# Six of eight output-projection chunks as three pairs of seven block products

## The chip, the cores and the metric

The kernel runs on one core of one Trainium2 chip. The metric is the device time of one execution in microseconds, as the median of three runs.

## The reference, cut to what matters

Two decoder layers work on `x` of 1024 tokens by 1024 features, all in float32. The part of a layer that the change touches is the output projection of the mixer and the addition to the residual stream, between the gated merge and the second RMSNorm:

```python
merged = g_a * (o_a @ w_br[l, :OUT_A]) + g_b * (o_b @ w_br[l, OUT_A:])
x = x + merged @ w_o[l]            # w_o[l] is 1024 x 1024
h2 = rmsnorm(x, norm2[l])
up = h2 @ w_up[l]
```

## The kernel before

Activations lie transposed: features on the 128 partitions, tokens along the free axis. The tokens are cut into two halves `n` = 0 and 1 of 512, the 1024 features into eight chunks of 128 (`k` on the input side, `e` on the output side). A float32 product is made of three float32r matmuls: every operand is split into a high part (`hh`, `w_hi`, cast by ScalarE at line 129) and a low part (`hl`, `w_lo`, the rest, subtracted by VectorE at line 130), and TensorE adds high times high, high times low and low times high in PSUM. A chunk of 128 output features for 512 tokens is therefore 8 times 3 = 24 matmuls of 128x512.

The merged activations are made by the loop at the end of `mixer`: for each of 16 (n, e) VectorE forms `mrg` (line 1279), ScalarE casts it into `hh` and GpSimd subtracts the low part into `hl` (`merged`, lines 1237 and 1238). Then comes the output projection: `wo_chunk` runs for the eight chunks of n = 0 and then for the eight of n = 1. It loads the chunk's weights in two pieces of 128x512, has them split, lets TensorE make 24 matmuls into a PSUM tile `o_ps`, adds the tile into `x` on VectorE (line 1128) and adds the square of the new `x` to the sum `nrm` for the RMSNorm (`norm_add`: ScalarE squares; VectorE adds for e = 1, 4 and 7, GpSimd for the others).

`norm(0, ...)` is the RMSNorm of the first half: four matmuls by ones give `nrm_t`, ScalarE takes the root, VectorE the reciprocal, four matmuls spread it over the partitions (`nrm_b`), and then for each of eight chunks VectorE scales `x` (line 479), ScalarE casts and VectorE or GpSimd subtracts the low part. `drive` weaves this into the chunks: 36 steps of `wo_chunk` run first (nine chunks), and 2.5 steps run for each step of the norm. The second half's norm is woven into the first products of the feed-forward network (`u_ps`).

TensorE's instructions stand in the order in which the program is written; on the other engines and on SyncE, which issues the DMAs, a scheduler sets the order at build time. On the chip every engine takes its own queue strictly in order. Buffers are rings with fixed counts: the split pieces `w_hi` and `w_lo` four each, raw weights `w_raw` two, the PSUM tag `ps` two, the temporaries of 128x512 (`mrg`, `sq` and others) six.

The feed-forward network and the q, k, v and gate projections already use a scheme of seven block products in place of eight (`seven`, lines 886 to 893, twelve matmuls a product); their sums of weight blocks are made by GpSimd (lines 1011 to 1018 in `pair_rest`), and three-step sums of activations as well (`block_sums`, lines 912 to 914).

Of the kernel before, what the change touches and what calls it, by code (L numbers as in the profile page):

```python
# [52 lines left out]
def trunk_kernel(ctx, tc, x, norm1, w_in, b_gate, w_br, w_o, norm2, w_up, conv_w, conv_b, w_down, norm_f, out, depth=None, probe=None):  # L53
# [62 lines left out]
    def bank(tag, name):  # L116
        return ps.tile([P, 512], F32, tag=tag, name=name)
# [15 lines left out]
    def weights(src, cols, place=None):  # L133

        per = 512 // cols
        got = []
        src = src.rearrange("(k p) n -> p k n", p=P)
        for r in range(0, KD, per):
            raw = sb.tile([P, per, cols], F32, tag="wr", bufs=NRAW, name="w_raw")
            nc.sync.dma_start(raw, src[:, r : r + per, :])  # L140
            if place:
                hi, lo = (x.rearrange("p (k c) -> p k c", c=cols)[:, r : r + per, :] for x in place)
            else:
                hi = sb.tile([P, per, cols], F32R, tag="wh", bufs=4, name="w_hi")
                lo = sb.tile([P, per, cols], F32R, tag="wl", bufs=4, name="w_lo")
            split(hi, lo, raw)
            got += [(hi[:, i, :], lo[:, i, :]) for i in range(per)]
        return got

    def product(o, pairs, first=True, last=True, share=False):  # L150

        n = len(pairs)
        quantum = 2 * 512 // o.shape[-1]
        for i, ((lh, ll), (rh, rl)) in enumerate(pairs):
            pe.matmul(o, lh, rh, start=(first and i == 0), stop=False, skip_group_check=share)  # L155
            pe.matmul(o, lh, rl, start=False, stop=False, skip_group_check=share)  # L156
            pe.matmul(o, ll, rh, start=False, stop=(last and i == n - 1), skip_group_check=share)  # L157
            if i % quantum == quantum - 1 and i < n - 1:
                yield
# [217 lines left out]
    def h_part(n, k):  # L377
        return H[n][0][:, k, :], H[n][1][:, k, :]
# [30 lines left out]
    def norm_add(n, e, first=False, sub=slice(0, HF), adds=None):  # L409

        if first:
            ACC[n] = sb.tile([P, HF], F32, tag="ql", bufs=2, name="nrm")
        acc = ACC[n]
        acc = acc[:, sub]
        sq = acc if first else small("sq")[:, sub]
        act.activation(sq, xc(n, e, sub), AF.Square)
        if not first:
            (adds or (dve if e % 3 == 1 else pool)).tensor_tensor(acc, acc, sq, ALU.add)
# [701 lines left out]
        return pair(dense, l, (OFF_G + e * P, OFF_G + D + e * P), False, put)  # L1120


    def wo_chunk(l, n, e):
        w = weights(w_o[l][:, e * P : (e + 1) * P], P)
        yield
        o = bank("ps", "o_ps")
        yield from product(o, [(w[k], h_part(n, k)) for k in range(KD)])
        dve.tensor_tensor(xc(n, e), xc(n, e), o, ALU.add)
        norm_add(n, e, e == 0)
        yield  # L1130

    def residual_in():

# [12 lines left out]
    def mixer(l, pending):  # L1146
# [79 lines left out]
        def branch_in(i):  # L1226
            if i < len(todo):
# [5 lines left out]
                    split(*parts_[q], raw[:, 2 * q : 2 * q + 2, :])  # L1233
                wbs.append(parts_)

        def merged(n, e, m):
            act.copy(H[n][0][:, e, :], m)
# [3 lines left out]
        wo = [wo_chunk(l, n, e) for n in range(2) for e in range(KD)]  # L1241

        for i in range(3):
            gate_in(i)
# [10 lines left out]
        for i, ab in order:  # L1255
            n, e = todo[i]
            sl = slice(n * HF, (n + 1) * HF)
            if i not in seen:
                if e == 0:
                    new_h(n)  # L1260
                if i % 4 == 0:
                    wb = wbs.pop(0)
                if l and i in X_AT:
                    x_in(X_AT.index(i) // 2, X_AT.index(i) % 2)
            gt = gts[i]
            ec = slice((e % 2) * P, (e % 2 + 1) * P)
# [12 lines left out]
            dve.tensor_tensor(m, gt[:, 0, :], gt[:, 1, :], ALU.add)  # L1279
            late.append((n, e, m))  # L1280
            if i == 11:
                next(wo[0])
# [8 lines left out]
            pass  # L1291
        table(AF.Sqrt, gt[:, 1, 0:1])
        S.clear()

        def first_half():
# [579 lines left out]
```

## Time and profile before

| | |
|---|---|
| runs | 2716.20, 2717.23, 2718.05 us; median 2717.23 us |
| the profiled execution | 2714.47 us, its span 2712.6 us, so 1.9 us lie around the span |
| TensorE | busy 2657.8 us of the span (98%), granted clock 0.997 |
| weight loads beside the matmuls | 2227.5 us (82%) |
| VectorE, ScalarE, GpSimd | 2105.9 (78%), 1330.4 (49%), 742.1 us (27%) |
| output projection, layer 0 | first matmul at 629.1 us, the last chunk added at 718.38 us |
| output projection, layer 1 | first matmul at 1969.34 us, last 2058.0 us |

Busy time is a sum over instructions; matmuls overlap, so the pace of TensorE is read from the distance of events, not from the duration of one matmul. A row of the timeline names the start, the duration, the engine, the line and the tiles, and in brackets how long the engine had been idle and for whom.

### The profile page before, as it was taken

How to read it: one execution, taken by the hardware profiler on the slowest of the kernel's cores; microseconds unless marked ns; L12 is line 12 of the kernel's file. 1: busy time of each engine (PE TensorE's matmuls, PEld its weight loads, DVE VectorE, ACT ScalarE, POOL GpSimd, SP SyncE). 2: the span in 40 equal slices, each digit the busy share in tenths (PEclk: the TensorE clock that was granted, in tenths of full speed). 3: DMA queues.
4: the chain of work that ended last, by engine and by line, in shares of the span. 5: the costliest groups of instructions: out<-in, count | busy, mean ns of one | idle time of the engine just before them, and what ended most of it. 6: DMA issues, size and time to landing. Idle time of an engine off the chain costs nothing. (4 is left out here: it accounts for less than half of the span.)

```text
span 2712.6 us, 37003 instructions
## 1 busy us (share of the span) xinstructions
PE 2657.8 (98%) x13098; PEld 2227.5 (82%) x13098; DVE 2105.9 (78%) x3104; ACT 1330.4 (49%) x2458; POOL 742.1 (27%) x537
## 2 busy tenths in 40 slices
PE   8999999999999999999999989999999999999999
PEld 8877788888888888888888778888788888888888
DVE  6877876675789988897658888766858888998865
ACT  5656534464455555432335665434545545554225
POOL 2004133322233434321220041332212433443210
PEclk9999999999999999999999999999999999999999
DMA  4023389863235444688401234997722444446863
GB/s 153 20 80 123 123 229 246 207 226 121 85 117 171 141 154 147 223 320 320 154 32 36 84 111 136 250 230 211 248 85 79 148 152 143 171 141 253 333 246 122
DMA packets 397637, 445.72 MB, mean 164 GB/s; under 512 B 21660, under 2 KB 318988, under 8 KB 395916
## 3 DMA queue, kind: packets, MB, share of 16 engines
q1 hardware_dynamic: 397452, 443.35, 51.4%
q8 instruction: 104, 1.70, 0.3%
q14 instruction: 81, 0.66, 0.1%
HBM read 300.61 MB, written 142.67 MB: 163 GB/s over the span
## 5 line engine op out<-in xcount | busy, mean ns | idle before, releaser
L130 DVE TENSOR_TENSOR w_lo<-up_a,w_hi 128x512 fp32r<-128x512 f32 x240 | 237.2, 995 | 20.5 <-ACT w_hi L129 20.5
L129 ACT CAST w_hi<-up_a 128x512 fp32r<-128x512 f32 x240 | 149.5, 623 | 184.1 <-PE u_a L890 45.6
L1631 DVE TENSOR_TENSOR x<-x,d_ps 128x512 f32<-128x512 f32 (+1 forms) x228 | 152.2, 672 | 76.9 <-PE d_ps L1625 76.0
L1362 POOL TENSOR_TENSOR cv<-cv 128x512 f32<-128x512 f32 x88 | 132.1, 1513 | 248.8 <-DVE cv L1357 138.9
L130 DVE TENSOR_TENSOR w_lo<-w_raw,w_hi 128x512 fp32r<-128x512 f32 x176 | 132.5, 756 | 67.8 <-ACT w_hi L129 67.3
L129 ACT CAST w_hi<-w_raw 128x512 fp32r<-128x512 f32 x176 | 109.2, 621 | 125.9 <-PE o_ps L156 68.6
L129 ACT CAST w_hi<-in_a 128x512 fp32r<-128x512 f32 x140 | 86.8, 620 | 147.6 <-PE i_a L890 83.2
L130 DVE TENSOR_TENSOR g<-cv,g 128x512 fp32r<-128x512 f32 x154 | 152.4, 991 | 5.2 <-ACT g L129 2.7
L1623 PE MATMUL d_ps<-gd_in,w_hi 128*128 128x512 f32 (+1 forms) x340 | 130.2, 383 | 1.3 <-ACT w_hi L129 1.1
L1625 PE MATMUL d_ps<-gd_in,w_lo 128*128 128x512 f32 (+1 forms) x340 | 129.8, 382 | 0.0
L1624 PE MATMUL d_ps<-gd_in,w_hi 128*128 128x512 f32 (+1 forms) x340 | 129.7, 382 | 0.0
L889 PE MATMUL u_a<-hh,w_hi 128*128 128x512 f32 x320 | 124.7, 390 | 0.5 <-DVE u L1513 0.5
L889 PE MATMUL u_a<-t_hi,w_hi 128*128 128x512 f32 x320 | 124.6, 389 | 0.0
L891 PE MATMUL u_a<-t_hi,w_lo 128*128 128x512 f32 x320 | 124.5, 389 | 0.0
L890 PE MATMUL u_a<-hl,w_hi 128*128 128x512 f32 x320 | 124.5, 389 | 0.0
L891 PE MATMUL u_a<-hh,w_lo 128*128 128x512 f32 x320 | 124.5, 389 | 0.0
L890 PE MATMUL u_a<-t_lo,w_hi 128*128 128x512 f32 x320 | 124.5, 389 | 0.0
L130 DVE TENSOR_TENSOR w_lo<-in_a,w_hi 128x512 fp32r<-128x512 f32 x140 | 116.0, 828 | 4.1 <-ACT w_hi L129 3.7
L1018 POOL TENSOR_TENSOR in_a<-in_a 128x512 f32<-128x512 f32 x28 | 38.0, 1357 | 278.9 <-DVE w_lo L130 278.9
L627 DVE TENSOR_TENSOR_SCAN stay<-stay,zero 128x128 f32<-128x128 f32 (+3 forms) x64 | 89.0, 1390 | 32.2 <-ACT stay L625 31.6
L1623 PE MATMUL d_ps<-gd_in,wd 128*128 128x512 f32 (+1 forms) x292 | 113.9, 390 | 0.0
L129 ACT CAST g<-cv 128x512 fp32r<-128x512 f32 x154 | 95.0, 617 | 38.2 <-POOL cv L1362 29.7
(390 smaller groups left out, 8747.7 us busy)
## 6 DMA issues: line engine op xcount, KB each, us to landing
gd<-g SPq DMA_DIRECT2D x154, 512.0 KB, 3.7
gd_in<-gd SPq DMA_DIRECT2D x154, 512.0 KB, 6.4
up_a<-in_w_up_dram SPq DMA_DIRECT2D x80, 512.0 KB, 5.8
in_a<-in_w_in_dram SPq DMA_DIRECT2D x56, 512.0 KB, 6.2
w_raw<-in_w_in_dram SPq DMA_DIRECT2D x104, 256.0 KB, 3.0
t_kq<-tk SPq DMA_DIRECT2D x64, 384.0 KB, 7.8
wd_raw<-in_w_down_dram SPq DMA_DIRECT2D x22, 1024.0 KB, 13.0
gin<-gs SPq DMA_DIRECT2D x32, 512.0 KB, 4.4
```

What stands on the lines that cost most here:

```text
L129: act.copy(hi, src)
L130: dve.tensor_tensor(lo, src, f32(hi), ALU.subtract)
L627: dve.tensor_tensor_scan(rev, rev, zero[:, 0:1].to_broadcast([P, L]), 1.0, ALU.mult, ALU.add)
L889: pe.matmul(o, w[0][:, c], rh, start=(first and i == 0), stop=False, skip_group_check=True)
L890: pe.matmul(o, w[0][:, c], rl, start=False, stop=False, skip_group_check=True)
L891: pe.matmul(o, w[1][:, c], rh, start=False, stop=(last and i == 3), skip_group_check=True)
L1018: pool.tensor_tensor(a11, a22, a11, ALU.subtract)
L1362: return lambda: pool.tensor_tensor(dst, a, b, ALU.subtract)
L1623: pe.matmul(o[:, sub], wh[:, c], gh[:, sub], start=(i == 0 and k in (0, 4, 5)), stop=False, skip_group_check=True)
L1624: pe.matmul(o[:, sub], wh[:, c], gl[:, sub], start=False, stop=False, skip_group_check=True)
L1625: pe.matmul(o[:, sub], wl[:, c], gh[:, sub], start=False, stop=(i == m - 1), skip_group_check=True)
L1631: dve.tensor_tensor(x, x, o[:, sub], ALU.add)
```

## The change

`output_products` replaces `wo_chunk`. Chunks 0 to 5 are taken as three pairs (2p, 2p+1). A pair for both halves of the tokens is a product of 2 by 2 blocks (512 input features by 128 output features each), made of seven products of twelve matmuls in place of eight. Chunks 6 and 7 stay plain. Every product is added from PSUM into each `x` chunk to which it belongs, so a product may be added twice.

Sums of weight blocks (`weight_sums`, four per pair) are made by GpSimd. Sums of activation blocks (`merged_sums`) are made in four rounds: the first while the activations are merged (GpSimd, in `merged`), the second and the fourth by VectorE, the third by GpSimd in three steps for each of four blocks; each round is then split into a high and a low part on ScalarE and VectorE. A `plan` hangs these tasks on the numbers of the products. The products stand in the order of `items`, numbered from 0: six halves of chunks 6 and 7 (0 to 5), then p1 and p3 of pairs 0 and 1 (6 to 9), p2 (10, 11), p5, p6 and so on to 22; this is `early`, which runs before the first half's norm. The six of `rest` (p2 of pair 2, the three p4, and the second half's chunk 7) are woven into that norm at 0.7 steps a step, with none ahead. The first half's sum `nrm` shares one buffer with the second's. The pieces of weights of an item are prepared three items ahead.

```diff
+    def output_products(l, sums):
+        b11, b12, b21, b22 = (lambda n=n, k=k: half(n, k) for k in range(2) for n in (1, 0))
+        def load_pairs():
+            for p in range(3):
+                if p < 2:
+                    t = [sb.tile([P, 2, HF], F32, tag="p4", bufs=4, name="wo_c") for _ in range(2)]
+                else:
+                    both = sb.tile([P, 4, HF], F32, tag="ql", bufs=2, name="wo_p")
+                    t = [both[:, 0:2, :], both[:, 2:4, :]]
...
+        def weight_sums(p):
+            a11, a12, a21, a22 = tiles[p]
+            pool.tensor_tensor(a21, a21, a22, ALU.add)
+            pool.tensor_tensor(a11, a21, a11, ALU.subtract)
+            pool.tensor_tensor(a12, a12, a11, ALU.subtract)
+            pool.tensor_tensor(a22, a22, a11, ALU.subtract)
+        def add(n, e, o, full=False):
+            dve.tensor_tensor(xc(n, e), xc(n, e), o, ALU.add)
+            if full:
+                norm_add(n, e, e == 6)
...
+        def p3(p):
+            items.append((("tile", p, 1), free("o_3"), p, b22, True, True, lambda o: add(0, 2 * p, o)))
+        def p5(p):
+            def done(o):
+                add(0, 2 * p + 1, o)
+                add(0, 2 * p, o, p == 2)
+            items.append((("tile", p, 2), free("o_5"), p, lambda: S[1], True, True, done))
+        def p7(p):
+            items.append((("tile", p, 3), again, p, lambda: S[3], False, True, lambda o: add(0, 2 * p + 1, o, True)))
...
+        chunk(0, 6)
+        chunk(0, 7)
+        chunk(1, 6)
+        for f, p in ((p1, 0), (p3, 0), (p1, 1), (p3, 1), (p2, 0), (p2, 1)):
+            f(p)
+        for f, p in ((p5, 0), (p6, 0), (p5, 1), (p6, 1), (p1, 2), (p7, 0), (p3, 2), (p7, 1), (p6, 2), (p5, 2), (p7, 2)):
+            f(p)
+        count = len(items)
+        for f, p in ((p2, 2), (p4, 0), (p4, 1), (p4, 2)):
+            f(p)
+        chunk(1, 7)
...
+        def prepare(i):
+            kind, c, k = items[i][0]
+            ready[i] = piece(loaded.pop(i) if kind == "raw" else tiles[c][k])
+            if kind == "tile" and k == 0 and items[i][4]:
+                weight_sums(c)
...
+        def run(first, last):
+            for i in range(first, last):
+                until("fetch", fetch, i + 5)
+                until("prepare", prepare, i + 3)
+                for f in sums.pop(i, ()):
+                    f()
...
+        def third(i):
+            r, (ah, al), (bh, bl) = small("h_sum"), half(0, 1)[i], half(0, 0)[i]
+            pool.tensor_tensor(r, f32(al), f32(bl), ALU.subtract)
+            pool.tensor_tensor(r, r, f32(ah), ALU.add)
+            pool.tensor_tensor(r, r, f32(bh), ALU.subtract)
...
+        for i in range(4):
+            task(i // 2, lambda i=i: split_into(1, i, keep[i]))
+            task(2 + i, second, i)
+            task(6 + 2 * i, third, i)
+            task(8 + 2 * i, lambda i=i: split_into(3, i, third_r[i]))
+            task(16 + i, fourth, i)
+            task(22, lambda i=i: split_into(4, i, keep[i]))
...
         def merged(n, e, m):
+            if e < 4:
...
+                    pool.tensor_tensor(sums[e], kept.pop((0, e)), kept.pop((1, e)), ALU.subtract)
...
-        drive(first_half(), relay(*wo, primed=True), 2.5, 36)
+        start, early, rest = output_products(l, merged_sums(sums))
+        start()
+        for _ in early():
+            pass
...
+        drive(first_half(), rest(), 0.7)
```

Three places of the instruction order show what the build makes of it, all in layer 0. The first is GpSimd's queue at the start of the output projection. Before, the last low parts of the merge are followed only by sums for the norm:

```order
L1238 TENSOR_TENSOR hl0_5946<-mrg_6378,hh0_5945 128x512
L1238 TENSOR_TENSOR hl0_5946<-mrg_6408,hh0_5945 128x512
L1238 TENSOR_TENSOR hl1_5964<-mrg_6436,hh1_5963 128x512
L1238 TENSOR_TENSOR hl1_5964<-mrg_6462,hh1_5963 128x512
L418 TENSOR_TENSOR nrm_6514<-nrm_6514,sq_6595 128x512
L418 TENSOR_TENSOR nrm_6514<-nrm_6514,sq_6636 128x512
```

Now the weight sums of pairs 0 and 1 (`wo_c_6471` and `wo_c_6472` are chunks 0 and 1, `wo_c_6475` and `wo_c_6476` chunks 2 and 3) and the third round (`h_sum`) stand there in one row:

```order
L1149 TENSOR_TENSOR wo_c_6472<-wo_c_6472,wo_c_6471 128x512
L1271 TENSOR_TENSOR h_sum_6655<-hl0_5946 128x512
L1271 TENSOR_TENSOR h_sum_6701<-hl0_5946 128x512
L1272 TENSOR_TENSOR h_sum_6655<-h_sum_6655,hh0_5945 128x512
L1272 TENSOR_TENSOR h_sum_6701<-h_sum_6701,hh0_5945 128x512
L1273 TENSOR_TENSOR h_sum_6655<-h_sum_6655,hh0_5945 128x512
L1273 TENSOR_TENSOR h_sum_6701<-h_sum_6701,hh0_5945 128x512
L1271 TENSOR_TENSOR h_sum_6743<-hl0_5946 128x512
L1147 TENSOR_TENSOR wo_c_6475<-wo_c_6476,wo_c_6475 128x512
L1272 TENSOR_TENSOR h_sum_6743<-h_sum_6743,hh0_5945 128x512
L1148 TENSOR_TENSOR wo_c_6475<-wo_c_6475 128x512
L1149 TENSOR_TENSOR wo_c_6476<-wo_c_6476,wo_c_6475 128x512
```

Ahead of these twelve stand L1147 and L1148 of `wo_c_6471`, of which the first overwrites the block that product 6 is split from. The eleventh row here, L1148 of `wo_c_6475`, makes the block that product 9 (p3 of pair 1) multiplies by; from L1147 of `wo_c_6471` to it are thirteen sums, eight of them of the third round, and the second row after it is the last `h_sum_6743`.

The second place is VectorE's queue around the same products. Before, a chunk has two splits, an addition from `o_ps` and sometimes a sum for the norm:

```order
L1128 TENSOR_TENSOR x0_5939<-x0_5939,o_ps_6528 128x512
L130 TENSOR_TENSOR w_lo_6566<-w_raw_6563,w_hi_6565 128x512
L418 TENSOR_TENSOR nrm_6514<-nrm_6514,sq_6554 128x512
L130 TENSOR_TENSOR w_lo_6601<-w_raw_6598,w_hi_6600 128x512
L1128 TENSOR_TENSOR x0_5939<-x0_5939,o_ps_6569 128x512
L130 TENSOR_TENSOR w_lo_6607<-w_raw_6604,w_hi_6606 128x512
L130 TENSOR_TENSOR w_lo_6642<-w_raw_6639,w_hi_6641 128x512
L1128 TENSOR_TENSOR x0_5939<-x0_5939,o_ps_6610 128x512
```

Now the low parts of the third round (`t_lo_6698` from `h_sum`), parts of the fourth (`m_sum`, L1278 and L1279), the additions from PSUM (L1152) and the splits of weights alternate; `o_ps_6609` is product 5's tile, `o_3_6679` product 7's, `w_lo_6676` belongs to product 9, `w_lo_6694` to product 10:

```order
L130 TENSOR_TENSOR t_lo_6698<-h_sum_6701,t_hi_6697 128x512
L1279 TENSOR_TENSOR m_sum_6074<-m_sum_6074,hl1_5964 128x512
L1152 TENSOR_TENSOR x1_5942<-x1_5942,o_ps_6609 128x512
L130 TENSOR_TENSOR w_lo_6676<-wo_c_6475,w_hi_6675 128x512
L130 TENSOR_TENSOR t_lo_6698<-h_sum_6743,t_hi_6697 128x512
L1278 TENSOR_TENSOR m_sum_6074<-hh1_5963,m_sum_6074 128x512
L1152 TENSOR_TENSOR x1_5941<-x1_5941,o_a_6659 128x512
L130 TENSOR_TENSOR w_lo_6694<-w_raw_6645,w_hi_6693 128x512
L1279 TENSOR_TENSOR m_sum_6074<-m_sum_6074,hl1_5964 128x512
L1278 TENSOR_TENSOR m_sum_6208<-hh1_5963,m_sum_6208 128x512
L1278 TENSOR_TENSOR m_sum_6242<-hh1_5963,m_sum_6242 128x512
L1152 TENSOR_TENSOR x0_5939<-x0_5939,o_3_6679 128x512
```

The addition of product 7's tile, which frees its PSUM bank, has moved behind the split of `h_sum_6743`, and that waits for two more sums on GpSimd.

The third place is TensorE's queue around the first half's norm. Before, `nrm_t` stands in the middle of the second half's chunk 1:

```order
L157 MATMUL o_ps_6856<-hh1_5963,w_lo_6806 128x512
L155 MATMUL o_ps_6856<-hh1_5963,w_hi_6805 128x512
L156 MATMUL o_ps_6856<-hl1_5964,w_hi_6805 128x512
L157 MATMUL o_ps_6856<-hh1_5963,w_lo_6806 128x512
L465 MATMUL nrm_t_6869<-ones_71,nrm_6514 128x1 x4
L155 MATMUL o_ps_6856<-hh1_5963,w_hi_6811 128x512
L156 MATMUL o_ps_6856<-hl1_5964,w_hi_6811 128x512
```

Now it stands right behind the last matmul of product 22, the last that adds into the first half:

```order
L893 MATMUL o_a_6881<-t_hi_6697,w_lo_6964 128x512
L891 MATMUL o_a_6881<-t_hi_6697,w_hi_6963 128x512
L892 MATMUL o_a_6881<-t_lo_6698,w_hi_6963 128x512
L893 MATMUL o_a_6881<-t_hi_6697,w_lo_6964 128x512
L467 MATMUL nrm_t_7037<-ones_71,nrm_6547 128x1 x4
L891 MATMUL o_2_7048<-hh1_5963,w_hi_6982 128x512
L892 MATMUL o_2_7048<-hl1_5964,w_hi_6982 128x512
```

What was a chunk and a half of the other half between the last addition into the first half and `nrm_t` is gone from there.

More of the change, by code (lines that the diff above doesn't have):

```diff
@@ L411, in norm_add @@
         if first:
-            ACC[n] = sb.tile([P, HF], F32, tag="ql", bufs=2, name="nrm")
+            if n == 0 or ACC[0] is None:
+                both = sb.tile([P, 2, HF], F32, tag="ql", bufs=2, name="nrm")
+                ACC[0], ACC[1] = both[:, 0, :], both[:, 1, :]
         acc = ACC[n]
@@ L1240, in mixer @@
         residual = residual_in() if l == 0 else iter(())
-        wo = [wo_chunk(l, n, e) for n in range(2) for e in range(KD)]
         for i in range(3):
@@ L1280, in mixer @@
             late.append((n, e, m))
-            if i == 11:
-                next(wo[0])
             if len(late) > 1:
@@ L1293, in mixer @@
         S.clear()
+        ACC[0] = None
+        start, early, rest = output_products(l, merged_sums(sums))
+        start()
+        for _ in early():
+            pass
         def first_half():
```

91 lines of the change are left out of this document (83 added, 8 removed).

## The prediction, as it was put on record

> **What bounds the kernel now.** I read first the busy times of the page, then the windows of the two output projections (columns: window, length, then busy time with count for PE, PEld, DVE, ACT and POOL, clock, DMA share, GB/s), then single rows of the timeline.
>
> ```profile
> PE 2657.8 (98%) x13098; PEld 2227.5 (82%) x13098; DVE 2105.9 (78%) x3104; ACT 1330.4 (49%) x2458; POOL 742.1 (27%) x537
> 629.10:680.90 51.80, 51.80 (x231) 42.94 (x230) 22.49 (x32) 19.47 (x31) 7.88 (x7) 1.00 0.30 87
> 718.20:760.00 41.80, 41.04 (x187) 33.48 (x186) 39.55 (x66) 24.84 (x42) 3.89 (x3) 1.00 0.22 67
> ```
>
> TensorE has no gap in the projection, and the others have room: VectorE 22.5 of 51.8 us, GpSimd 7.9. Right behind it, in the second norm, VectorE is full (39.55 of 41.8) and TensorE idles 0.76 us. So every matmul taken out of the projection is worth its time, as long as the others keep TensorE fed.
>
> ```profile
> L155 PE MATMUL o_ps<-hh,w_hi x256: 389/389/486, 629.1 to 2057.6; 128*128 128x512 f32 x128
> 1969.34 0.39 PE L155 MATMUL o_ps<-hh,w_hi 128*128 128x512 f32 x1
> 640.34 0.69 DVE L1128 TENSOR_TENSOR x<-x,o_ps 128x512 f32<-128x512 f32 x1 [1.55 <-PE o_ps L157]
> 645.78 0.69 DVE L1128 TENSOR_TENSOR x<-x,o_ps 128x512 f32<-128x512 f32 x1 [1.56 <-PE o_ps L157]
> ```
>
> One matmul lasts 389 ns, but VectorE, waiting for TensorE both times, gets a chunk of 24 every 645.78 - 640.34 = 5.44 us: 0.2267 us a matmul, 2.72 us for a product of twelve.
>
> **What is removed.** A layer had 16 x 24 = 384 projection matmuls and has 3 x 7 x 12 + 4 x 24 = 348. That is 36 fewer, 8.2 us a layer, **16.3 us in both**. The duration of 389 ns would have made it 28.0 us, and the sum below 11.7 us lower. The Trainium skill (Trainium Kernel Development and Optimization, Performance Expectations) calls matmul busy time a bad metric, because matmuls are pipelined; the trace agrees.
>
> **What is added and hidden.** Per layer VectorE gets twelve more additions from PSUM, 16 sums of activations and 16 more splits, and loses three weight splits: 41 operations of 0.6 to 0.7 us, some 26 us. By the window it has 29 us free in the first 52, so it fits if it comes in time. ScalarE's 13 more casts of 0.62 us are hidden likewise. The weights are 6 loads of 512 KB and 14 of 256 KB, 6.5 MB where it was 8. In the merge GpSimd takes four more subtractions; it has gaps there, and I count nothing, with 1 us a layer as the bound if VectorE has to wait for a `mrg` buffer.
>
> **The first wait: GpSimd's thirteen sums.** GpSimd was nearly idle here; now it decides when product 9 can start.
>
> ```profile
> 258.35 3.43 POOL L914 TENSOR_TENSOR h_sum<-h_sum,hh 128x512 f32<-128x512 f32 x2
> 261.75 1.29 POOL L912 TENSOR_TENSOR h_sum<-hl,hl 128x512 f32<-128x512 f32 x1
> 263.12 1.29 POOL L913 TENSOR_TENSOR h_sum<-h_sum,hh 128x512 f32<-128x512 f32 x1
> 264.49 1.29 POOL L914 TENSOR_TENSOR h_sum<-h_sum,hh 128x512 f32<-128x512 f32 x1
> 265.73 1.29 POOL L912 TENSOR_TENSOR h_sum<-hl,hl 128x512 f32<-128x512 f32 x1
> L914 POOL TENSOR_TENSOR h_sum<-h_sum,hh 128x512 f32<-128x512 f32 x16 | 24.2, 1525 | 0.3
> L913 POOL TENSOR_TENSOR h_sum<-h_sum,hh 128x512 f32<-128x512 f32 x16 | 22.7, 1434 | 0.3
> L1011 POOL TENSOR_TENSOR in_a<-in_a 128x512 f32<-128x512 f32 x28 | 37.8, 1351 | 111.9 <-DMA in_a<-in_w_in_dram 111.8
> 672.80 0.62 ACT L129 CAST w_hi<-w_raw 128x512 fp32r<-128x512 f32 x1 [2.10 <-PE o_ps L156]
> 698.52 0.68 DVE L130 TENSOR_TENSOR w_lo<-w_raw,w_hi 128x512 fp32r<-128x512 f32 x1
> 699.12 0.68 DVE L482 TENSOR_TENSOR hl<-b_f,hh 128x512 fp32r<-128x512 f32 x1
> 699.72 0.73 DVE L479 SCALAR_TENSOR_TENSOR b_f<-x,g,nrm_b 128x512 f32<-128x512 f32 x1
> ```
>
> A sum on GpSimd takes 1.24 to 1.37 us from start to start when left alone and up to 3.43/2 = 1.72 beside a busy VectorE; the groups' means lie between 1.35 and 1.53, and I take 1.45, since VectorE is busier here than before. VectorE starts an operation every 0.60 us when nothing holds it.
>
> Layer 0, counted from 629.1. Product 6 is split into the buffers of product 2, free at 629.1 + 3 x 2.72 = 637.3. Cast (0.62, and 0.1 for the handover) and split take until 639.1, and only then may L1147 overwrite product 6's block. Thirteen sums later, at 639.1 + 13 x 1.45 = 658.0, the block of product 9 is there; its cast ends at 658.8. TensorE, having run on, would want it at 629.1 + 9 x 2.72 = 653.6. **Product 9 starts 5.2 us late.**
>
> It does not end there, because VectorE's queue is tied to the same sums. The split of `h_sum_6743` needs two more (660.9) and a cast (661.6), and as the seventh operation of 0.60 behind it stands the addition that frees the PSUM bank of product 7 for product 10: 661.7 + 0.6 + 7 x 0.6 = 666.5. Product 10, ready to follow at 661.5, starts at 666.6. Product 11 needs the bank of product 9, freed six operations later, at 670.2; planned was 629.1 + 11 x 2.72 = 659.0. The layer has then lost **11.3 us**. After that VectorE has two or three operations per product of 2.72 us, and GpSimd's later sums have several products' time, so I see no third loss. At 1.30 us a sum the loss is 8.9, at 1.65 it is 14.3.
>
> ```profile
> 629.86 1.24 DVE L1279 TENSOR_TENSOR mrg<-gin 128x512 f32<-128x512 f32 x1
> 1971.13 1.71 DVE L1279 TENSOR_TENSOR mrg<-gin 128x512 f32<-128x512 f32 x1
> gin<-gs SPq DMA_DIRECT2D x32, 512.0 KB, 4.4
> in_a<-in_w_in_dram SPq DMA_DIRECT2D x56, 512.0 KB, 6.2
> ```
>
> The last of these weights (512 KB) waits for the buffer of the last merge. In layer 0 that ends at 631.1, 1.9 us behind the first projection matmul; 4.4 to 6.2 us of loading end before 639. In layer 1 it ends at 1972.84, 3.5 us behind 1969.34, plus some 1.5 us for the first round's splits now put into VectorE's full queue there: landing at 1978.7 or later, then one sum, against 1979.3 when L1147 could start. That is about 1 us more: **12.3 us** in layer 1.
>
> **The second wait: `nrm_t` without cover.**
>
> ```profile
> 712.94 0.69 DVE L1128 TENSOR_TENSOR x<-x,o_ps 128x512 f32<-128x512 f32 x1 [1.55 <-PE o_ps L157]
> 713.66 0.63 ACT L416 ACTIVATE sq<-x 128x512 f32<-128x512 f32 x1 [0.28 <-DVE x L1128]
> 714.44 1.56 POOL L418 TENSOR_TENSOR nrm<-nrm,sq 128x512 f32<-128x512 f32 x1 [4.15 <-ACT sq L416]
> ```
>
> From the last matmul of a chunk to the end of its sum on GpSimd is 716.00 - 712.94 plus the handover, some 3.2 us. Before, 36 matmuls of the other half covered it; now product 22 ends with the same chain (chunk 5, GpSimd adds) and nothing stands between. With VectorE's older work, **3.3 us a layer**; behind `nrm_t` stands all of TensorE's queue.
>
> **The third wait: the second half's `nrm_t`.**
>
> ```profile
> 689.78 1.41 DVE L479 SCALAR_TENSOR_TENSOR b_f<-x,g,nrm_b 128x512 f32<-128x512 f32 x2 [1.09 <-PE nrm_b L474]
> ...
> 702.09 1.13 DVE L482 TENSOR_TENSOR hl<-b_f,hh 128x512 fp32r<-128x512 f32 x1
> 718.38 0.69 DVE L1128 TENSOR_TENSOR x<-x,o_ps 128x512 f32<-128x512 f32 x1 [1.24 <-PE o_ps L157]
> 720.19 0.68 DVE L418 TENSOR_TENSOR nrm<-nrm,sq 128x512 f32<-128x512 f32 x1
> ```
>
> The first half's norm takes VectorE from 689.78 to 703.2 with 20 operations, 0.67 each. The cover behind `nrm_b` shrinks from 126 matmuls to 60, 13.6 us. VectorE now has 17 operations there (11.4 us), so the first half's activations are in time; but ten more, the next sums of activations, stand ahead of the addition of the last chunk, which so comes about 4 us after its matmuls instead of at once (718.38), and the sum that `nrm_t` waits for (720.19 before) with it. Bounds 0 and 4.5; I take **3.0 us a layer**.
>
> **The sum.** -16.3 + 11.3 + 12.3 + 2 x 3.3 + 2 x 3.0 = +19.9 us. Against the profiled execution's 2714.47 (span 2712.6 and 1.9 around it) that is 2734.4. The median of the runs, 2717.23, is 2.8 us above that execution, so the time is **2737 us**.
>
> **The rivals.**
>
> *The order holds and TensorE stays fed.* Then only the uncovered `nrm_t` costs: -16.3 + 6.6 = -9.7, 2707.5 us, faster. For it: TensorE lives with a VectorE that is 95% full behind the projection. It decides where thirteen sums fit into 653.6 - 639.1 - 0.8 = 13.7 us, 1.05 us each; no row of GpSimd's 128x512 sums is that short. Chance 0.10.
>
> *The first wait stays single.* Product 9 is late by 5.2 us a layer, but VectorE catches up before it holds a bank: -16.3 + 10.4 + 6.6 + 3 = +3.7, 2721 us, within what can be told. It needs the split of `h_sum_6743` not to hold the queue; but its sum stands two places behind the block's. Chance 0.10.
>
> *The two engines lock each other out.*
>
> ```profile
> L130 DVE TENSOR_TENSOR w_lo<-w_raw,w_hi 128x512 fp32r<-128x512 f32 x18 | 13.1, 727 | 14.2 <-ACT w_hi L129 14.2
> L130 DVE TENSOR_TENSOR w_lo<-up_a,w_hi 128x512 fp32r<-128x512 f32 x107 | 108.8, 1023 | 5.7 <-ACT w_hi L129 5.7
> ```
>
> The split takes 727 ns in the projection and 1023 in the feed-forward network, where GpSimd works beside it. If an operation of VectorE with both inputs in SBUF never runs beside a sum of GpSimd, the products 0 to 22, with 31 sums on GpSimd and 55 such operations on VectorE by the order, need 31 x 1.29 + 55 x 0.6 = 73.0 us of the two against 276 x 0.2267 = 62.6 on TensorE: 10.4 us lost a layer, spread evenly and not at products 9 to 11; -16.3 + 20.8 + 6.6 + 6 = +17.1, 2734 us. Against it: the queues' waits above come first and leave both engines idle time. Chance 0.08. The Trainium skill (SBUF — State Buffer, Who interferes with whom) says that a VectorE instruction with two SBUF inputs contends with a GpSimd instruction that reads SBUF, and that the one that comes second blocks; the two rows agree in kind.
>
> **How the numbers follow.** My forecast, with all three waits, has 0.72. Its own bounds: sums at 1.30 and no third wait, -16.3 + 8.9 + 9.9 + 6.6 = +9.1 (2726); sums at 1.65, 4.5 us at the third wait and 2 for the merge, -16.3 + 14.3 + 15.3 + 6.6 + 9 + 2 = +30.9 (2748). The range takes in the single wait below and leaves the fast rival out: 2716 to 2748. A difference under 0.2%, 5.4 us, can't be told from none. Faster by more: 0.10. Within: most of the second rival and a little of the forecast, 0.09. Slower: 0.81.
>
> **What would show it.** Right: TensorE idles some 5 us ahead of product 9 (released by ScalarE's cast, behind GpSimd), again ahead of 10 for VectorE's addition, and 3 us ahead of each `nrm_t`; GpSimd is busy without a gap for 19 us before. Wrong, if TensorE has no gap before product 12: then GpSimd's sums are shorter or start earlier than I count. Wrong in size, if the gaps ahead of products 10 and 11 are under 2 us, or if the merge or products 13 to 22 show gaps that I don't have.

## The result: slower by 62 us, and the profile after

The changed kernel takes 2778.69 us (median of four runs, 2774.53 to 2783.72) against 2716.72 us before: a ratio of 1.0231, 95% interval 1.0214 to 1.0248. The direction was forecast, the size was not: +62 us instead of +20, outside the range. The profiled execution after is the longest of the four, 2783.72 us, its span 2781.9.

The page's first row after, and the windows from the last merge matmul to the first `u_a` of the feed-forward network, layer by layer, before and after (columns: window, length, busy time with count of PE, PEld, DVE, ACT, POOL, then granted clock, DMA share, GB/s):

```profile
PE 2675.2 (96%) x13026; PEld 2232.8 (80%) x13026; DVE 2182.6 (78%) x3186; ACT 1343.6 (48%) x2484; POOL 829.5 (30%) x593
```

```profile
629.00:765.10 136.10, 135.34 (x613) 111.82 (x612) 92.59 (x143) 63.32 (x104) 24.76 (x18) 1.00 0.27 82
1969.50:2105.20 135.70, 134.93 (x610) 111.42 (x609) 93.81 (x145) 63.59 (x105) 25.74 (x18) 1.00 0.28 82
```

```profile
631.90:797.00 165.10, 140.46 (x577) 112.47 (x575) 130.69 (x183) 67.71 (x114) 63.23 (x42) 0.92 0.17 50
2006.10:2172.40 166.30, 141.22 (x573) 112.51 (x572) 132.33 (x186) 68.13 (x114) 60.98 (x41) 0.91 0.16 47
```

The two stages are 59.6 us longer, of 69.3 us between the two profiled executions (2714.47 and 2783.72). Of the other 9.7 us, 2.9 lie in the two merges; the rest lies in parts that the change doesn't touch, where the execution after has more stretches at half the clock (one of 10.2 us at 8.4 us, where the one before has none), and is not explained further. Idle time of TensorE (length minus busy) was 0.8 us in each; now it is 24.6 and 25.1, together **48.2 us** more. And busy time has grown by 5.1 and 6.3 us although 36 matmuls of 0.2267 us are gone in each, so that the other matmuls ran **27.7 us** slower. 48.2 + 27.7 - 16.3 = 59.6. The granted clock, 1.00 before, says where most of the 27.7 come from: by the clock's records 60 and 64 matmuls started while it stood at one half, and at 0.2 us each they would make 24.8 of it. That is a count; what the clock costs in time is tested below.

TensorE's timeline after, layer 0: the rows with a wait, in brackets its length and its releaser.

```profile
644.77 0.47 PE L891 MATMUL o_ps<-hh,w_hi 128*128 128x512 f32 x1 [1.52 <-DVE x L1152]
660.54 0.79 PE L893 MATMUL o_a<-hh,w_lo 128*128 128x512 f32 x1 [3.67 <-DVE w_lo L130]
...
661.56 0.63 PE L892 MATMUL o_a<-hl,w_hi 128*128 128x512 f32 x1
661.99 0.63 PE L893 MATMUL o_a<-hh,w_lo 128*128 128x512 f32 x1
...
669.82 0.80 PE L891 MATMUL o<-hh,w_hi 128*128 128x512 f32 x1 [5.22 <-ACT w_hi L129]
677.75 0.77 PE L891 MATMUL o<-hh,w_hi 128*128 128x512 f32 x1 [2.81 <-DVE x L1152]
718.24 1.75 PE L467 MATMUL nrm_t<-ones,nrm 128*128 128x1 f32 x8 [3.41 <-POOL nrm L420]
742.52 0.50 PE L157 MATMUL u_ps<-hh,w_lo 128*128 128x512 f32 x1 [1.59 <-DVE w_lo L130]
750.33 1.83 PE L467 MATMUL nrm_t<-ones,nrm 128*128 128x1 f32 x8 [5.24 <-DVE nrm L420]
```

The waits in the products stand ahead of 4, 8, 9 and 10 (13.2 us; 11.3 were forecast, ahead of 9 to 11), the first half's `nrm_t` (3.41; forecast 3.3) and the second half's (5.24; forecast 3.0). The 1.59 us ahead of the feed-forward network's first product (`u_ps`) had not been forecast. The two rows between have no wait, yet start 0.43 us apart instead of 0.23. Windows at those places:

```profile
656.90:660.40 3.50, 0.00 (x0) 0.00 (x0) 3.50 (x3) 0.00 (x0) 3.50 (x3) 1.00 0.00 0
660.40:663.80 3.40, 3.26 (x8) 2.58 (x9) 1.45 (x3) 1.24 (x2) 3.40 (x3) 0.50 0.00 0
...
718.40:725.20 6.80, 6.80 (x21) 5.64 (x22) 0.18 (x1) 0.50 (x2) 0.00 (x0) 0.50 0.09 26
749.10:755.90 6.80, 5.58 (x17) 4.83 (x18) 1.95 (x4) 2.35 (x4) 0.00 (x0) 0.50 0.27 80
```

Behind these waits the granted clock is one half for 3.4 us or a multiple of it. My sum had no term for that at all. GpSimd's and VectorE's timelines from 637 us on show the other thing that it missed:

```profile
647.77 2.82 POOL L1147 TENSOR_TENSOR wo_c<-wo_c 128x512 f32<-128x512 f32 x1 [5.50 <-issue]
...
653.18 3.42 POOL L1271 TENSOR_TENSOR h_sum<-hl 128x512 f32<-128x512 f32 x2
656.56 3.37 POOL L1272 TENSOR_TENSOR h_sum<-h_sum,hh 128x512 f32<-128x512 f32 x2
...
666.19 1.71 POOL L1272 TENSOR_TENSOR h_sum<-h_sum,hh 128x512 f32<-128x512 f32 x1
667.86 1.26 POOL L1148 TENSOR_TENSOR wo_c<-wo_c 128x512 f32<-128x512 f32 x1
```

```profile
637.05 3.47 DVE L1265 TENSOR_TENSOR m_sum<-hh,m_sum 128x512 f32<-128x512 f32 x2
...
645.15 0.68 DVE L130 TENSOR_TENSOR w_lo<-w_raw,w_hi 128x512 fp32r<-128x512 f32 x1
...
646.96 0.68 DVE L130 TENSOR_TENSOR w_lo<-wo_c,w_hi 128x512 fp32r<-128x512 f32 x1
...
653.68 1.77 DVE L130 TENSOR_TENSOR t_lo<-m_sum,t_hi 128x512 fp32r<-128x512 f32 x1
655.38 1.77 DVE L420 TENSOR_TENSOR nrm<-nrm,sq 128x512 f32<-128x512 f32 x1
657.07 1.75 DVE L1278 TENSOR_TENSOR m_sum<-hh,m_sum 128x512 f32<-128x512 f32 x1
658.74 1.74 DVE L130 TENSOR_TENSOR w_lo<-wo_c,w_hi 128x512 fp32r<-128x512 f32 x1
...
666.70 0.68 DVE L1152 TENSOR_TENSOR x<-x,o_ps 128x512 f32<-128x512 f32 x1
```

From 653 us on VectorE's operations with two inputs in SBUF start 1.69 us apart, and so do GpSimd's sums: the two engines take turns. The addition at 666.70, which has one input in PSUM, takes its usual 0.68 beside a sum. At 645.15, with GpSimd idle, the same kind of split takes 0.68.

### The profile page after: what moved, and what is told of

Same layout as the page of the kernel before. It is cut to its first block, busy times and chain, and to the rows that moved or that the text cites. A ratio compares the mean times of both kernels' runs of the same rounds, so it can differ in the third digit from the quotient of the medians.

```text
span 2781.9 us, 36907 instructions
## 1 busy us (share of the span) xinstructions
PE 2675.2 (96%) x13026; PEld 2232.8 (80%) x13026; DVE 2182.6 (78%) x3186; ACT 1343.6 (48%) x2484; POOL 829.5 (30%) x593
## 3 DMA queue, kind: packets, MB, share of 16 engines
q8 instruction: 103, 1.69, 0.3%
## 5 line engine op out<-in xcount | busy, mean ns | idle before, releaser
L130 DVE TENSOR_TENSOR w_lo<-w_raw,w_hi 128x512 fp32r<-128x512 f32 x140 | 105.5, 759 | 30.9 <-ACT w_hi L129 30.5
L420 POOL TENSOR_TENSOR nrm<-nrm,sq 128x512 f32<-128x512 f32 x29 | 40.8, 1406 | 255.8 <-ACT sq L418 255.1
L129 ACT CAST w_hi<-w_raw 128x512 fp32r<-128x512 f32 x140 | 86.4, 620 | 60.7 <-PE r_ps L156 15.8
```

The source lines that it names most:

```text
L129: act.copy(hi, src)
L130: dve.tensor_tensor(lo, src, f32(hi), ALU.subtract)
```

## The experiments

Theory A: TensorE waits, and each long wait also costs clock. For the waits in the products there are two readings: Q, the forecast's, that products wait for GpSimd's sums in its queue; and L, the lock: GpSimd's sums hold VectorE, whose splits and additions come late. Times of one group stand beside runs of the kernel before on the same chip (2716.65 to 2718.05 us).

### The products: queue or lock

The sums left out, in the first kernel:

```diff
         def weight_sums(p):
-            pool.tensor_tensor(a21, a21, a22, ALU.add)
...
+            pass
...
-            pool.tensor_tensor(r, r, f32(bh), ALU.subtract)
-            third_r[i] = r
+            third_r[i] = f32(half(0, 1)[i][0])
```

> The changed kernel without GpSimd's 24 sums a layer in the projection: the weights' sums are left out (the blocks are used as loaded), and the third round of activations is split from one block of the merged half instead of from the sum of three. The splits, additions, loads and matmuls stay. Theory A (products 8 to 10 wait for GpSimd, and VectorE is slowed by it): the gaps ahead of products 8, 9 and 10 go (11.7 us in layer 0, 12.5 us in layer 1) with the 51 matmuls at half clock behind them (10 us): 34 us less, 2744 (2738 to 2750), and VectorE's operations of two SBUF inputs take 0.60 us each from start to start instead of 1.7. Theory C (VectorE's own 41 further operations make the waits, GpSimd or not): more than half of these gaps stays, 2761 or more.

2739.54 us (2735.31 to 2742.22), 39 less. All waits of the 23 products went, but for one of 1.74 us in layer 1; the waits ahead of the `nrm_t` stayed at 3.41 and 5.25. So the sums are to blame, by their time on GpSimd or by being waited for. Then the same sums, read by nobody:

```diff
+            r = small("unread")
+            pool.tensor_tensor(r, a21, a22, ALU.add)
...
-            third_r[i] = r
+            third_r[i] = f32(half(0, 1)[i][0])
```

> GpSimd does the same 24 sums a layer at the same places of its queue, but into buffers that nothing reads; products and splits use the blocks as loaded, as in the kernel without GpSimd's sums (2739.5). So no product waits for a sum, and GpSimd still works beside VectorE. Theory Q (the products waited for the thirteen sums in GpSimd's queue): 2739.5 within 4 us. Theory L (each sum also holds VectorE's operations of two SBUF inputs for 1.09 us, 24 x 1.09 = 26 us a layer, and VectorE's queue comes late for the products): gaps at VectorE's splits and additions, 2748 to 2765.

2773.52 us (2770.44 to 2776.47): with no product waiting for a sum, 34.0 of the 39.2 us are back, and the time lies above L's own range, so L had been priced too low. As the only cause Q falls: the lock alone is enough for most of the loss. No run has the queue without the lock, so what the wait for the thirteen sums would cost by itself stays open. Of the 34.0 some 9.6 us are clock, by the count above: 120 matmuls started at half the clock here, 72 without the sums. The split of `wo_c`, by kernel, from the groups of lines (between the bars stand the busy us and the mean ns of one; unread, then without GpSimd's sums):

```profile
L130 DVE TENSOR_TENSOR w_lo<-wo_c,w_hi 128x512 fp32r<-128x512 f32 x20 | 23.2, 1160 | 0.0
```

```profile
L130 DVE TENSOR_TENSOR w_lo<-wo_c,w_hi 128x512 fp32r<-128x512 f32 x20 | 13.7, 683 | 0.0
```

The same operations of VectorE, in the windows of the two stages (unread, then without GpSimd's sums):

```profile
630.30:791.40 161.10, 138.64 (x578) 110.93 (x576) 137.56 (x184) 67.78 (x114) 64.62 (x42) 0.94 0.18 53
2000.80:2166.60 165.80, 141.33 (x572) 113.07 (x572) 138.22 (x186) 68.05 (x115) 64.38 (x42) 0.92 0.16 47
```

```profile
630.40:774.40 144.00, 133.42 (x576) 109.28 (x575) 116.72 (x184) 67.97 (x114) 25.65 (x18) 0.95 0.21 59
1986.00:2132.90 146.90, 133.94 (x573) 109.06 (x573) 119.19 (x185) 67.95 (x115) 25.67 (x18) 0.95 0.18 53
```

VectorE is busy 20.8 and 19.0 us longer for the same work. The waits in layer 0 with the sums unread are now spread over the products, most of them released by VectorE:

```profile
651.15 0.50 PE L893 MATMUL o_a<-hh,w_lo 128*128 128x512 f32 x1 [1.58 <-DVE w_lo L130]
656.90 0.47 PE L891 MATMUL o<-hh,w_hi 128*128 128x512 f32 x1 [3.17 <-ACT t_hi L129]
663.56 0.50 PE L893 MATMUL o_a<-hh,w_lo 128*128 128x512 f32 x1 [1.06 <-DVE w_lo L130]
668.25 0.47 PE L891 MATMUL o<-hh,w_hi 128*128 128x512 f32 x1 [2.10 <-DVE x L1153]
```

The unread sums take buffers from the same ring of six as the squares. That did not hold VectorE: in layer 0 it has no idle time at all from 629.4 to 679 us, so it was late by the length of its operations. The reverse test keeps the 24 sums, on VectorE. It takes away lock and queue together, so it can't tell them apart; it asks whether VectorE's own load is the cause.

```diff
-            pool.tensor_tensor(a21, a21, a22, ALU.add)
+            dve.tensor_tensor(a21, a21, a22, ALU.add)
...
-            pool.tensor_tensor(r, f32(al), f32(bl), ALU.subtract)
+            dve.tensor_tensor(r, f32(al), f32(bl), ALU.subtract)
```

> The changed kernel with GpSimd's 24 sums a layer in the projection (12 of weights, 12 of activations) on VectorE instead. Theory A with the lock (beside a sum on GpSimd a VectorE operation of two SBUF inputs takes 1.69 us from start to start instead of 0.60, so that a sum on GpSimd costs VectorE 1.09 us, and one on VectorE 0.60): the gaps ahead of products 8 to 10 shrink to a third or less, and the half clock behind them with it, 20 to 34 us less: 2750 (2744 to 2758). Theory C (VectorE's own queue is what TensorE waits for, and 14.4 us more in it make that worse): 2779 or more, with the gaps ahead of products that wait for an addition.

2745.99 us (2743.02 to 2748.33), 33 less, with 24 more operations on VectorE. Its windows of the two stages:

```profile
630.60:781.20 150.60, 135.50 (x577) 109.64 (x576) 135.03 (x208) 67.82 (x115) 27.40 (x18) 0.94 0.20 57
1988.20:2139.40 151.20, 135.99 (x574) 110.40 (x573) 135.52 (x209) 67.69 (x114) 27.64 (x18) 0.93 0.17 52
```

VectorE is busy 135.0 us with 208 operations, and was 130.7 with 183: doing the sums itself costs it hardly more than being held by them. Where both queues are full (653 to 660 us after), a sum on GpSimd takes 1.69 - 0.60 = 1.09 us out of VectorE's queue, a sum on VectorE 0.60. Over the two stages together the two cost VectorE about the same: 24 sums a layer add 0.83 us each to its busy time when GpSimd makes them unread, 0.72 when VectorE makes them itself. The waits in the products are down to 1.5 and 2.6 us, but the one ahead of the first half's `nrm_t` has grown from 3.41 to 5.74 and 5.55:

```profile
702.01 1.87 PE L467 MATMUL nrm_t<-ones,nrm 128*128 128x1 f32 x8 [5.74 <-POOL nrm L420]
```

The Trainium skill (SBUF — State Buffer, Who interferes with whom) states that a VectorE instruction with two SBUF inputs contends with a GpSimd instruction that reads SBUF, and that one with at most one SBUF input, outside the two-port modes, doesn't; both halves agree with VectorE's rows after (1.77 and 0.68 us).

### The clock

> The changed kernel with 14 matmuls of no use ahead of the first nrm_t of a layer's second norm and 22 ahead of its second one; they write the same PSUM bank, which nrm_t then overwrites, so every wait stays and only TensorE is no longer idle in it. Theory A (the two waits cost 3.4 + 5.2 us a layer, and behind each the granted clock stays at one half for 6.8 us, where 73 matmuls of both layers take 0.43 us instead of 0.23): the half clock at 718, 749, 2094 and 2125 us is gone, and the time falls by 73 x 0.2 = 14.6 us, to 2764 (2760 to 2768). Theory B (the waits alone are the loss and the clock in the records costs nothing): no change, 2776 to 2782, or some us more.

```diff
         tot = bank(tag, "nrm_t")
+        for _ in range(fill):
+            pe.matmul(tot, H[n][0][:, 0, 0:P], H[n][0][:, 0, :], start=True, stop=True, skip_group_check=True)
```

2768.24 us (2765.13 to 2768.78), 10.5 less than the changed kernel for 72 matmuls more, and no half clock is left behind either `nrm_t`. The two stages, in which the waits of the products were not filled:

```profile
630.90:790.80 159.90, 144.00 (x613) 115.50 (x613) 129.98 (x184) 68.62 (x116) 65.24 (x42) 0.94 0.17 51
1998.70:2157.20 158.50, 142.05 (x609) 113.67 (x608) 130.18 (x185) 68.08 (x114) 63.20 (x41) 0.95 0.17 50
```

In this pair of executions the stages are 5.2 and 7.8 us shorter, 13.0 against the 14.6 expected. So the clock costs time, theory B falls, and the medians give 10.5 of the 14.6 counted. The price of one wait in an otherwise unchanged kernel was harder to get. In the kernel before I put `nrm_t` right behind its last chunk:

```diff
-        drive(first_half(), relay(*wo, primed=True), 2.5, 36)
+        drive(first_half(), relay(*wo, primed=True), 2.5, 30)
```

> The kernel before with one number changed, so that nrm_t of the first half stands right behind the first half's last chunk; the 36 matmuls that covered it follow it. Nothing else is moved. Theory A: a gap of 3.2 to 3.4 us in each layer, 6.6 us, and in the 3.4 to 6.8 us behind it half the clock, 2 to 4 us a layer: 2716.7 + 6.6 + 4 to 8 = 2727 to 2731. Theory B: 2716.7 + 6.6 = 2723, no half clock behind the gap.

2722.28 us (ten runs, 2719.81 to 2727.46) against 2718.05: the gap was 2.24 us, not 3.3, and half the clock followed in one layer of two. The 4.2 us are no more than the two gaps, 4.5.

```profile
677.16 1.05 PE L465 MATMUL nrm_t<-ones,nrm 128*128 128x1 f32 x8 [2.24 <-DVE nrm L418]
```

> The same with 14 matmuls of no use (3.2 us) in the gap, into the bank that nrm_t overwrites. Theory A: the clock stays whole and the time is 2716.7 + 6.6 = 2723, 4 to 8 us below the kernel with the bare gap. Theory B: the same time as with the bare gap.

2725.67 us: the 3.2 us of matmuls were longer than the gap, and the pair says nothing. With the last square on GpSimd the gap is 2.85 us. This kernel was run twice; the first time 3.4 us of gap had been expected, with 2731.5 us for theory A and 2724.5 for B, and 2728.32 us came, between the two.

```diff
-        norm_add(n, e, e == 0)
+        norm_add(n, e, e == 0, adds=pool if n == 0 and e == 7 else None)
```

> The kernel before with the bare first nrm_t and the last square added by GpSimd once more, for its trace. If the gap is 3.4 us and half the clock follows for 3.4 to 6.8 us in both layers, the time is 2728 to 2732, and the pair before was blurred by scatter. If the gap is short or no half clock follows, it is 2724 to 2728 and the clock costs nothing here.

> The same with 15 matmuls of no use (3.4 us) in the gap. Theory A: no half clock, 2717.6 + 6.8 = 2724.5 (2722 to 2727), some 7 us below the kernel without them. Theory B: no difference.

2727.37 us bare, 2727.57 filled: no difference. Eight matmuls a layer ran at half the clock, 1.6 us, and the matmuls of no use were 0.55 us longer than the gap; such a difference is within the scatter of these runs. So the gap was made longer by two operations of GpSimd:

```diff
+            pool.tensor_tensor(q, ACC[0], xc(0, 0), ALU.add)
+            pool.tensor_tensor(ACC[0], q, xc(0, 0), ALU.subtract)
```

> The same with two further operations on GpSimd behind that addition (one of the activations added to the sum and subtracted again), so that the bare gap ahead of the first nrm_t is 2.6 us longer, some 6 us. Theory A: 2 x 6.0 us, and half the clock for 6.8 us behind each, 2 x 17 x 0.2 = 6.8 us: 2716.7 + 18.8 = 2735.5 (2732 to 2740). Theory B (the gaps alone): 2728.7 (2726 to 2731).

> The same with 26 matmuls of no use (5.9 us) in that gap. Theory A: the clock stays whole, 2716.7 + 12 = 2728.7, some 7 us below the kernel with the long bare gap. Theory B: no difference.

2733.68 us (2732.90 to 2735.45) against 2729.58 (2728.77 to 2730.90) with the gap filled: 4.1 us for two gaps, where A expected 7. Every one of the four bare runs is longer than every filled one. The layer 0 rows, bare and filled:

```profile
678.67 1.87 PE L465 MATMUL nrm_t<-ones,nrm 128*128 128x1 f32 x8 [5.52 <-POOL nrm L1133]
```

```profile
629.20:774.30 145.10, 138.81 (x613) 114.33 (x612) 93.94 (x142) 63.64 (x104) 26.90 (x20) 0.96 0.26 77
```

```profile
630.70:773.10 142.40, 141.23 (x638) 116.64 (x637) 93.78 (x142) 63.40 (x104) 27.01 (x20) 1.00 0.26 78
```

The clock costs time, then: 2 us for such a gap here, and 2.6 us for one of the four in the changed kernel. Both times less came back than the count of slow matmuls says (4.1 of 7, 10.5 of 14.6), and behind gaps of 2.24 and 2.85 us no cost could be told from the scatter. The 24.8 us counted in the changed kernel are therefore an upper figure.

### The second half's `nrm_t`

```diff
             yield from norm(0, g2[:, 0, :], "t", keep=True)
-            yield from first_sum()
-
         drive(first_half(), rest(), 0.7)
+        for _ in first_sum():
+            pass
```

> The changed kernel with the four sums of the first half's new activations (first_sum, four operations and four splits on VectorE) written behind the second half's last chunk instead of between the norm's steps. Theory A (nrm_t of the second half waits because eight operations stand ahead of the last chunk's addition in VectorE's queue): the gap of 5.2 us ahead of it goes in both layers, and the 35 matmuls at half clock behind it, 10.5 + 7 = 17.5 us: 2761 (2757 to 2766). Rival: the sums are needed early enough that the wait only moves to the products that read them: 2772 to 2779.

2769.60 us (2768.41 to 2778.38), 9 less instead of 17.5. In the changed kernel the second half's last addition stands at 747.70, 7.4 us behind its last matmul (the next product starts at 740.32):

```profile
740.32 0.39 PE L155 MATMUL u_ps<-hh,w_hi 128*128 128x512 f32 x1
747.70 0.68 DVE L1152 TENSOR_TENSOR x<-x,o_ps 128x512 f32<-128x512 f32 x1
```

With the sums behind it that distance is 2.6 us (738.99 to 741.55), and the wait ahead of `u_ps` falls from 1.59 to 0.38. TensorE's rows at the second norm in layer 0:

```profile
744.17 1.02 PE L467 MATMUL nrm_t<-ones,nrm 128*128 128x1 f32 x8 [1.63 <-DVE nrm L420]
751.22 1.98 PE L476 MATMUL nrm_b<-ident,ss 128*128 128x128 f32 x8 [3.15 <-DVE ss L470]
```

The wait of 5.24 us fell to 1.63, as the queue's reading has it, but a new one of 3.15 us came up ahead of `nrm_b`: the scheduler now puts the reciprocal (L470) behind the sums and a step of the feed-forward network's convolution. Both theories were half right.

### The edits put together

> Both edits together: the 24 sums on VectorE and first_sum behind the second half's last chunk. If the two losses are independent, as theory A has it, their gains add up: 2750 - 17.5 = 2733 (2726 to 2741), with the wait ahead of the first half's nrm_t (3.4 us and its half clock) as the main one left. If VectorE is then full through the whole stage, less than half of the second gain shows: 2742 or more.

2740.10 us (2736.48 to 2746.36), 5.9 below the sums on VectorE alone: inside theory A's range, but a third of the 17.5 us that it added up. The second edit alone had brought 9.1; the 3 us between are within the scatter of four runs, so whether the two measured gains add up is not shown.

```diff
-            pool.tensor_tensor(r, f32(al), f32(bl), ALU.subtract)
-            pool.tensor_tensor(r, r, f32(ah), ALU.add)
-            pool.tensor_tensor(r, r, f32(bh), ALU.subtract)
+            dve.tensor_tensor(r, keep[i], f32(bh), ALU.subtract)
+            dve.tensor_tensor(r, r, f32(bl), ALU.subtract)
...
-            task(2 + i, second, i)
+            task(4 + i, second, i)
```

> As the kernel with both edits, and with the third round of activations made from the second (second round less b11, two operations instead of three), the first and second round two products later, the third three. Theory A with the lock: eight operations of 0.60 us a layer less on VectorE in both layers at most give 5 us where VectorE is the bound: 2728 (2722 to 2736). Rival (the order at the start is what counts, not the number): the gap ahead of product 4 goes (1.5 us a layer) and nothing else changes, some 3 us less than the kernel with both edits.

2740.85 us: neither theory's gain came, though four operations a layer are gone from VectorE. Then everything at once, and a higher priority for the reciprocal and for the squares of the second half (`first_sum` now runs in two steps behind the second half's `nrm_b`):

```diff
-        drive(first_half(), rest(), 0.7)
+        drive(first_half(), rest(), 0.7, 2)
...
-        drive(pending, before(steps, 2), 0.7, 2)
+        drive(pending, before(steps, 2), 0.5, 4)
...
+            if i in (4, 5):
+                next(sum_steps)
+                next(sum_steps)
```

> The changed kernel mended at each place that the runs have shown: the 24 sums on VectorE, the third round of activations from the second (8 operations, not 12), the rounds placed two to three products later, one product of the second half (12 matmuls) ahead of the first half's nrm_t, the first half's new sums behind the second half's nrm_b, and 24 matmuls of the next stage instead of 12 ahead of the second half's nrm_t. Theory A: -16.3 us of matmuls, 0.7 us ahead of the first nrm_t, 1 to 2 us ahead of the second and its nrm_b, 2 to 4 us of gaps in the products a layer and no gap over 2.7 us, so little half clock: 2714.5 - 16.3 + 2 x (0.7 + 1.5 + 3) + 3 = 2712 (2704 to 2722). Rival (VectorE is full over the stage with 107 operations of 0.60 us against 62.6 us of matmuls, and the waits come back elsewhere): 2725 to 2740.

2719.89 us (ten runs), 1.0011 times the kernel before (1.0002 to 1.0021). No wait over 1.8 us is left in the two stages.

```diff
-                    pool.tensor_tensor(sums[e], kept.pop((0, e)), kept.pop((1, e)), ALU.subtract)
+                    dve.tensor_tensor(sums[e], kept.pop((0, e)), kept.pop((1, e)), ALU.subtract)
...
-                norm_add(n, e, e == 6)
+                    norm_add(n, e, e == 6, adds=dve if (n, e) == (0, 5) else None)
```

> best3 with the four differences of the merge (m_sum) on VectorE instead of GpSimd, and with the first half's last square added by VectorE. Theory L (a sum on GpSimd costs VectorE 1.09 us, on VectorE 0.60): the merge of layer 1, 2.7 us longer than in the kernel before, loses 1 to 2 us of that, the gaps of 1.0 and 1.2 us ahead of the first nrm_t shrink to 0.4: 2716 (2712 to 2720), no more than the kernel before. Rival: VectorE is full there, and 2720 or more results.

2717.32 us (ten runs, 2710.57 to 2720.47), a ratio of 0.9997 (0.9988 to 1.0007): the kernel before, reached again and not beaten. Its windows say why:

```profile
629.70:764.70 135.00, 129.43 (x577) 104.62 (x576) 132.35 (x206) 68.23 (x116) 25.84 (x17) 1.00 0.21 61
1970.40:2106.40 136.00, 129.30 (x573) 103.94 (x572) 133.32 (x207) 67.80 (x115) 25.63 (x17) 1.00 0.20 59
```

The clock is whole and TensorE is busy 5.9 and 5.6 us less than before, but VectorE is busy 132.4 of 135.0 us, where it was 92.6 of 136.1. TensorE's waits, 5.6 and 6.7 us, now stand beside an engine that is nearly full. That VectorE is the bound is read from these rows and not shown: no run took work off it in this kernel.

## Why the prediction was wrong, point by point

The stages grew by 59.6 us where the sum had 19.9. Of the 39.7 us between, 27.7 are slower matmuls, which the sum had at nothing without giving a reason, and 12.0 are longer waits (48.2 against 36.2). The step that failed in size is the missing term for the clock; the step that failed in its cause is the first wait, where VectorE was taken as free beside GpSimd.

- **The matmuls removed, -16.3 us.** 36 a layer are gone, by the counts. In the one kernel whose clock is whole in both stages (best4) TensorE's busy time falls by 11.5 us, less than the 16.3. Its stages have eight and nine more gaps, and around a gap busy time grows: the matmul ahead counts with its whole 0.39 us, and the distance right behind is 0.31 us (644.77 to 645.08 after), not 0.2267.
- **The first wait, 11.3 + 12.3 us.** The size was near (13.2 us in layer 0, ahead of products 4 and 8 to 10; 13.8 in layer 1, ahead of 4 and 7 to 11), the cause in the main wrong: "VectorE starts an operation every 0.60 us when nothing holds it" was used for a queue that GpSimd holds, and so were the 29 us that VectorE had free. The split of product 6, put at 639.1, came at 646.96, behind a VectorE that had not been idle since 628.8 and had lost some 5.8 us of that taking turns with GpSimd (at 637.05 two operations take 3.47 us). GpSimd's thirteen sums then took from 647.77 to 669.1, 1.64 us each instead of 1.45. That they delay product 9 is true of the trace (5.22 us, by ScalarE's cast; that it is the 5.2 of the forecast is luck, since the sums ended and TensorE arrived some 11 us later than put). With nobody reading them the loss only moves to other products.
- **The signs.** All those named for "right" came: 5.22 us ahead of product 9 by ScalarE's cast, 2.81 ahead of 10 by VectorE's addition, 3.41 and 5.24 ahead of the `nrm_t`, GpSimd busy without a gap from 647.77 us on. They fit both accounts, so they could not tell the queue from the lock. The length of VectorE's splits would have told. The sign named for a wrong size came in part as well: no gap ahead of 11 in layer 0, 1.57 and 1.84 us ahead of 10 and 11 in layer 1. The gaps ahead of 4, 7 and 8 were in neither list.
- **The lock as a rival.** It had a chance of 0.08, since "the queues' waits above come first and leave both engines idle time". The runs show it as the cause of 34 us, 17 a layer, of which some 5 are clock by the count; the remaining 12 are near the 10.4 at which it was priced. So it was sized about right and given too little chance, and its sum of +17.1 misses the measured time by the clock as well.
- **The second wait, 3.3 us.** Right: 3.41 in both layers.
- **The third wait, 3.0 us with bounds of 0 and 4.5.** The mechanism is right (sum_last), the size was 5.24 and 5.25, above the bound: the last chunk's addition came 7.4 us after its matmuls, where I had put 4. Ahead of `u_ps` another 1.6 us a layer came that I had not seen.
- **The merge, nothing with a bound of 1 us a layer.** 0.4 us in layer 0 (51.1 to 51.5 us from its first to its last matmul), 2.5 us in layer 1 (44.7 to 47.2).
- **The clock, no term.** Of the 27.7 us of slower matmuls, 24.8 are half clock by the count; the filled gaps gave back 10.5 of 14.6 counted in the same way, so how much of the 27.7 is the clock's stays open between these two measures.
- **Slips in the sums.** The single-wait rival is added up with 3 us at the third wait where the forecast has 6, and the loss at 1.30 us a sum comes to 9.0, not 8.9. Neither bears on the outcome.

## What to carry to other kernels

Price a wait of TensorE as its length plus the slow matmuls behind it, and look in the trace of before for what the clock did behind its gaps. A sum moved to an idle GpSimd isn't free while VectorE works out of SBUF: here it cost VectorE about as much as doing it itself (0.83 and 0.72 us), and more where both queues were full (1.09 and 0.60). Name signs that tell the forecast from its rivals, not only signs that fit it. Count what a saving on the full engine adds to the next one: VectorE went from 93 to 131 us of the stage, and the best of the orders tried here is level with the kernel before.

## What had not been expected of the hardware

In 17 traces of this case (without the first 30 and the last 15 us of each), every one of 47 gaps of TensorE of 2.7 us or more was followed by half the granted clock within 3.5 us, or lay in it; of 101 gaps of 2.0 to 2.7 us 52, of 137 of 1.4 to 2.0 us 58, and of 464 shorter ones (over 0.4 us) 6. The half clock lasted 3.4 us or a multiple of that, and matmuls of 128x512 started 0.43 us apart in it. The same gap of 2.24 us in the same execution had it in one layer and not in the other (bare_norm). The Trainium skill (TensorE: Matmul & The Clock Gate, HAM oscillation — how this bites in real kernels) warns of idle gaps over about 3.4 us; the trace agrees above that, but half of the gaps of 2.0 to 2.7 us were enough here.
